# The last four experts write their rows of the output themselves, and the other rows are loaded beside them

## The chip, the cores and the metric

One core of a Trainium2 chip runs the whole program. The metric is the device time of one execution in microseconds. The kernel before takes 1597.99 us (median of 3 runs, 1597.9 to 1598.13).

## The reference

One decoder layer over 2048 tokens of width 1024, in float32: a gated-linear-attention mixer with a residual, then a mixture of experts with a residual, then a final RMSNorm. What matters here is the second half. Each token chooses one of 8 groups and, in it, 2 of 8 experts:

```python
hid = jax.nn.silu(xb @ w1[e]) * (xb @ w3[e])      # xb: the rows of expert e, 1024 -> 256
ys = (hid @ w2[e]) * slot_gate[:, None]           # 256 -> 1024
out = zeros.at[slot_tok].add(ys)                  # two experts a token
x = x + out
return rmsnorm(x, final_norm)                     # each row by its own mean square
```

With 64 experts and 4096 assignments, an expert has 64 rows on average. A row of the result can be normalised once both of its experts have been added.

## The kernel before

The first 930 us are attention and routing; the change does not touch them. They leave four things in DRAM or SBUF: `s["X"]`, the residual stream in DRAM; `s["h"]`, its normalised rows in DRAM; `tok`, a column per expert with the token numbers of its first 96 rows (a number past 2047 where there are fewer); and `s["gate"]`, the factors.

`phase_moe` runs iterations e = 0 to 64, expert by expert, in an order in which neighbours are of different groups (`ORDER`), so that 8 experts in a row share no token. The order of instructions on every engine is the order in which the program writes them. Iteration e scales and scatters the result of expert e-2 (`down` on ACT, `scatter`: an indirect DMA on POOL that adds rows into `s["X"]`), multiplies expert e by its first weights (`up`, twice 12 matmuls), transposes the hidden rows of e-1 (`htrans`), transposes the input rows of e+1 (`xtrans`), gathers the rows of e+4 (`gather`: an indirect DMA on POOL), splits the next weights into two parts (ACT makes the high part on L1157, DVE the low part on L1160), and multiplies expert e-1 by its second weights (`down_mm`, 12 matmuls). Weights come in pieces of 1 MB on SP's queue, up to 11 ahead, into 19 wide slots that `Experts` hands out (`fetch`, `split`, `use`).

An indirect DMA reads its row numbers from SBUF; POOL makes its descriptors, and the DMA engines carry the rows.

After the loop, `phase_more` is a loop over overflow blocks (experts with more than 96 rows); with these inputs it runs no iteration, but entering and leaving it is work for all engines. Then `phase_tail` loads all 16 tiles of `s["X"]` on SP's queue, takes mean squares on ACT (`square`, L1401), the inverse root with one Newton step (`root`, `refine`), multiplies on DVE (`norm`, L1422, with `gf`, the final norm's gain, in SBUF) and stores to `out` on SP's queue (L1423).

Lines that come up below: L67 is the low part of a split whose input is in PSUM, L1222 the product of the two halves of the hidden rows (one input in PSUM), L1004 the scatter of routing entries into a table, L1192 and L1246 the gather and the scatter-add of an expert.

Of the kernel before, what the change touches and what calls it, by code (L numbers as in the profile page):

```python
# [21 lines left out]
S = 2048  # L22
# [35 lines left out]
NTAIL = 29  # L58
# [1112 lines left out]
def phase_moe(tc, c, a, s, ex, plan, rest):  # L1171
    nc = tc.nc
    with ExitStack() as ctx:
# [10 lines left out]
        scat = []  # L1184
# [55 lines left out]

        def down(e):
            Y[e] = ys[e % YS]
            nc.scalar.activation(Y[e][0:CAP, :], PD[e][0:CAP, :], AF.Copy, scale=s["gate"][0:CAP, ORDER[e]:ORDER[e] + 1])  # L1243

        def scatter(e):
            st = nc.gpsimd.indirect_dma_start(  # L1246
                out=s["X"], out_offset=bass.IndirectOffsetOnAxis(ap=tok[:, ORDER[e]:ORDER[e] + 1], axis=0),
                in_=Y[e], in_offset=None, bounds_check=S - 1, oob_is_err=False, compute_op=OP.add)
            for i, o in enumerate(scat):
# [23 lines left out]
        for e in range(E + 1):  # L1273
            live = e < E
            if e > 1:
                down(e - 2)
                scatter(e - 2)
            if live:
                up(e, 0)
# [16 lines left out]
            if e:  # L1296
                down_mm(e - 1)
            if e == 2:
                s["plan"] = plan_more(tc, s, plan)
        down(E - 1)  # L1300
        scatter(E - 1)


def plan_more(tc, s, one):
# [25 lines left out]
    total = one.tile([1, 1], I32, name="total")  # L1330
    nc.vector.tensor_copy(total, end[0:1, E - 1:E])
# [4 lines left out]
def phase_more(tc, c, a, s, slots):  # L1336

    nc = tc.nc
    with ExitStack() as ctx:
        ps = ctx.enter_context(tc.tile_pool(name="o_ps", bufs=1, space=PSUM, reuse_waits="tile"))  # L1340
        ident = c["ident"]
        tl, total, tab = s["plan"]
        w = [slots.tile(F32) for _ in range(6)]
        x, xt, y, small = own = [slots.tile(F32) for _ in range(4)]
        hid, ht = small[:, 0:FF], small[:, FF:2 * FF]
        nc.vector.memset(x, 0.0)
        n = nc.values_load(total[0:1, 0:1], min_val=0, max_val=E)
        with tc.For_i(0, n, 1) as i:
            SP = [mybir.EngineType.SP]
            e = nc.values_load(tl[0:1, bass.ds(i * 2, 1)], engines=SP, min_val=0, max_val=E - 1)  # L1350
            b = nc.values_load(tl[0:1, bass.ds(i * 2 + 1, 1)], engines=SP, min_val=0, max_val=(SLOTS - CAP) // MORE - 1)
            for k in range(6):
                nc.sync.dma_start(w[k], a["w_moe"][bass.ds(e, 1), k // 2, :, k % 2 * D:(k % 2 + 1) * D].rearrange("o p f -> p (o f)"))
            nc.sync.dma_start(tab, s["table"][CAP * E:].rearrange("(b p e) w -> b p e w", p=MORE, e=E)[
                bass.ds(b, 1), :, bass.ds(e, 1), :].rearrange("b p e w -> p (b e w)"))
            nc.gpsimd.indirect_dma_start(
                out=x, out_offset=None, in_=s["h"], in_offset=bass.IndirectOffsetOnAxis(ap=tab[:, 0:1], axis=0),
                bounds_check=S - 1, oob_is_err=False)
            for j in range(2):
                p = ps.tile([128, 512], F32, name="p", bufs=2)  # L1360
                for k in range(4):
                    nc.tensor.transpose(p[:, k * 128:(k + 1) * 128], x[:, (4 * j + k) * 128:(4 * j + k + 1) * 128], ident)
                nc.scalar.activation(xt[:, j * 512:(j + 1) * 512], p, AF.Copy)
            pu = ps.tile([128, 512], F32, name="pu")
            for k in range(NK):
                nc.tensor.matmul(pu, xt[:, k * 128:(k + 1) * 128], w[k // 2][:, k % 2 * 512:(k % 2 + 1) * 512],
                                 start=(k == 0), stop=(k == NK - 1))
            nc.scalar.activation(hid, pu[:, 0:FF], AF.Silu)
            nc.vector.tensor_tensor(hid, hid, pu[:, FF:], op=OP.mult)
            p = ps.tile([128, 256], F32, name="pt")  # L1370
            for k in range(2):
                nc.tensor.transpose(p[:, k * 128:(k + 1) * 128], hid[:, k * 128:(k + 1) * 128], ident)
            nc.scalar.activation(ht, p, AF.Copy)
            for j in range(2):
                p = ps.tile([128, 512], F32, name="p", bufs=2)
                for k in range(2):
                    nc.tensor.matmul(p, ht[:, k * 128:(k + 1) * 128], w[4 + k][:, j * 512:(j + 1) * 512],
                                     start=(k == 0), stop=(k == 1))
                nc.scalar.activation(y[:, j * 512:(j + 1) * 512], p, AF.Copy, scale=tab[:, 1:2].bitcast(F32))
            nc.gpsimd.indirect_dma_start(  # L1380
                out=s["X"], out_offset=bass.IndirectOffsetOnAxis(ap=tab[:, 0:1], axis=0),
                in_=y, in_offset=None, bounds_check=S - 1, oob_is_err=False, compute_op=OP.add)
        slots.free(*w, *own)


def phase_tail(tc, c, a, s, slots, gf):
    nc = tc.nc
    GRP = 4
    with ExitStack() as ctx:
        sm = ctx.enter_context(tc.tile_pool(name="t_sm", bufs=2, side="right", reuse_waits="tile"))  # L1390
        junk = [slots.tile(F32) for _ in range(2)]
        X, SS, R = {}, {}, {}

        def load(t):
            X[t] = slots.tile(F32)
            nc.sync.dma_start(X[t], s["X"][t * 128:(t + 1) * 128, :])

        def square(t):
            if t % GRP == 0:
                SS[t // GRP] = sm.tile([128, GRP], F32, name="ssq")  # L1400
            nc.scalar.activation(junk[t % 2], X[t], AF.Square, accum_out=SS[t // GRP][:, t % GRP:t % GRP + 1])  # L1401

        def root(g):

            v = sm.tile([128, GRP], F32, name="v")
            nc.vector.tensor_scalar(v, SS[g], 1.0 / D, EPS, op0=OP.mult, op1=OP.add)
            y = sm.tile([128, GRP], F32, name="r")
            nc.scalar.activation(y, v, AF.Ln)
            nc.scalar.activation(y, y, AF.Exp, scale=-0.5)
            R[g] = v, y  # L1410

        def refine(g):
            v, y = R[g]
            u = sm.tile([128, GRP], F32, name="u")
            nc.vector.tensor_tensor(u, y, y, op=OP.mult)
            nc.vector.tensor_tensor(u, u, v, op=OP.mult)
            nc.vector.tensor_scalar(u, u, -0.5, 1.5, op0=OP.mult, op1=OP.add)
            nc.vector.tensor_tensor(y, y, u, op=OP.mult)

        def norm(t):  # L1420
            g, i = divmod(t, GRP)
            nc.vector.scalar_tensor_tensor(X[t], X[t], R[g][1][:, i:i + 1], gf, op0=OP.mult, op1=OP.mult)  # L1422
            nc.sync.dma_start(a["out"][t * 128:(t + 1) * 128, :], X[t])  # L1423

        NG = NT // GRP
        for t in range(NT):
            load(t)
        nc.scalar.preload_act_table_set(LN_EXP)
        for t in range(GRP):
            square(t)  # L1430
        root(0)
        refine(0)
        for t in range(GRP, 2 * GRP):
            square(t)
        for g in range(NG):
            if g + 1 < NG:
                root(g + 1)
                for t in range((g + 2) * GRP, min((g + 3) * GRP, NT)):
                    square(t)
            for i in range(GRP):  # L1440
                if i == GRP // 2 and g + 1 < NG:
                    refine(g + 1)
                norm(g * GRP + i)
# [3 lines left out]
def trunk(ctx, tc, a):  # L1447
# [7 lines left out]
        "todo": dram.tile([128, 2], I32, name="s_todo"),  # L1455
        "X": dram.tile([S, D], F32, name="s_X"),
# [22 lines left out]
    with ExitStack() as main:  # L1479
        big = main.enter_context(tc.tile_pool(name="tails", bufs=NTAIL, side="left", reuse_waits="tile"))  # L1480
        slots = Slots()
        slots.add(big, NTAIL)
        gf = slots.tile(F32)
        nc.sync.dma_start(gf, bass.AP(tensor=a["final_norm"].tensor, offset=a["final_norm"].offset, ap=[[0, 128], [1, D]]))
        phase_more(tc, c, a, s, slots)
        phase_tail(tc, c, a, s, slots, gf)
# [41 lines left out]
```

## Time and profile before

| what | value |
|---|---|
| timed runs, median | 1597.99 us |
| profiled execution | 1600.11 us |
| its span, first to last instruction | 1598.3 us |
| PE busy | 1514.1 us (95%) |
| DVE busy | 1096.7 us (69%) |
| ACT busy | 957.0 us (60%) |
| POOL busy | 365.9 us (23%) |
| granted TensorE clock, mean | 0.974 |

The busy shares are means over the whole span. The profile's rows are read by stage: attention and routing to about 930 us, the experts to 1546 us, the tail to the end. A row of an engine's timeline gives the start, the length and the instruction; what stands in brackets is the idle time ahead of it and what ended it. The end of an instruction of POOL that issues a DMA is the end of its descriptors, not the landing of the data.

### The profile page before, as it was taken

The numbers are of one execution on the slowest core, as the hardware profiler recorded it, in microseconds if no ns is written. First come the engines' busy times: TensorE is split into PE (matmuls) and PEld (weight loads), VectorE is DVE, ScalarE is ACT, GpSimd is POOL, SyncE is SP. The second block draws the span as 40 slices with busy tenths as digits, with TensorE's granted clock in tenths as the row PEclk, the third lists the DMA queues.
The fourth block names the chain that finished last, engine by engine and source line by source line (L and its number), as shares of the span: only waits on it lengthen the run. The fifth ranks groups of instructions, "written<-read, shape, count | busy, mean of one in ns | idle before, by whom it ended". The sixth has DMA issues, their size and how long they took to land.

```text
span 1598.3 us, 21450 instructions
## 1 busy us (share of the span) xinstructions
PE 1514.1 (95%) x7619; PEld 1197.2 (75%) x7619; DVE 1096.7 (69%) x2087; ACT 957.0 (60%) x1498; POOL 365.9 (23%) x265
## 2 busy tenths in 40 slices
PE   9999999999999999998999969999999999999960
PEld 7877888888888888877888856777777777777740
DVE  5566665566556655553655558889998998989955
ACT  6666644454445544441222238888888888888854
POOL 3211000000000000130111144535444444454320
PEclk9999999999999999999999979999999999999985
DMA  8645944434333433347488556999999999999969
GB/s 305 227 158 200 341 144 150 145 139 181 120 117 138 174 123 124 132 138 265 174 278 276 212 218 237 386 391 396 390 390 394 394 396 393 386 393 394 392 189 392
DMA packets 113213, 415.24 MB, mean 260 GB/s; under 512 B 23585, under 2 KB 40066, under 8 KB 88530
## 3 DMA queue, kind: packets, MB, share of 16 engines
q1 hardware_dynamic: 90242, 379.72, 61.3%
q0 software_dynamic: 19744, 33.85, 8.4%
q8 instruction: 60, 0.98, 0.2%
q10 hardware_dynamic: 3120, 0.30, 0.2%
q14 instruction: 47, 0.39, 0.1%
HBM read 353.92 MB, written 93.41 MB: 280 GB/s over the span
## 4 chain that ended last, share of the span: by engine, by line
PE 88%; DVE 5%; DMA 3%; ACT 2%; issue 1%; SPq 0%; POOL 0%; DVEq 0%; POOLq 0%; ACTq 0%
PE pm L832 9%; PE pu L77 7%; PE pu L76 7%; PE pu L75 7%; PE pvr L75 7%; PE pvr L76 7%; PE pvr L77 7%; PE pd L76 4%; PE pd L75 4%; PE pd L77 4%; PE ptr L1203 3%; PE pk L75 2%; PE pq L75 2%; PE pq L76 2%; PE pq L77 2%; PE pk L76 2%
## 5 line engine op out<-in xcount | busy, mean ns | idle before, releaser
L1160 DVE TENSOR_TENSOR wide<-wide 128x2048 fp32r<-128x2048 f32 x192 | 435.0, 2286 | 55.4 <-ACT wide L1157 46.8
L1157 ACT ACTIVATE wide<-wide 128x2048 fp32r<-128x2048 f32 x192 | 362.7, 1908 | 6.8 <-PE pd L76 6.4
L1246 POOL DMA_INDIRECT s_X<-y,tok x64 | 187.5, 2929 | 297.8 <-ACT y L1243 283.3
L75 PE MATMUL pu<-wide,xhi 128*96 128x512 f32 x512 | 207.0, 404 | 0.9 <-ACT xhi L66 0.9
L76 PE MATMUL pu<-wide,xhi 128*96 128x512 f32 x512 | 202.5, 396 | 2.2 <-DVE wide L1160 2.2
L77 PE MATMUL pu<-wide,xlo 128*96 128x512 f32 x512 | 203.6, 398 | 0.0
L75 PE MATMUL pvr<-big 128*128 128x512 f32 x504 | 201.2, 399 | 0.0
L76 PE MATMUL pvr<-big 128*128 128x512 f32 x504 | 197.1, 391 | 0.0
L77 PE MATMUL pvr<-big 128*128 128x512 f32 x504 | 196.8, 391 | 0.0
L832 PE MATMUL pm<-big 128*128 128x512 f32 x672 | 163.4, 399 | 5.4 <-DVE big L910 5.4
L67 POOL TENSOR_TENSOR big<-big 128x1024 fp32r<-128x1024 f32 x16 | 39.3, 2468 | 517.6 <-ACT big L66 458.2
L832 PEld LDWEIGHTS pm<-big 128*128 128x128 f32 x672 | 126.0, 191 | 31.4 <-DVE big L910 5.8
L77 PEld LDWEIGHTS pu<-wide,xlo 128*96 128x96 f32 x512 | 83.2, 162 | 36.7 <-DVE xlo L67 0.6
L75 PEld LDWEIGHTS pvr<-big 128*128 128x128 f32 x504 | 94.6, 188 | 20.5
L77 PEld LDWEIGHTS pvr<-big 128*128 128x128 f32 x504 | 94.6, 188 | 20.3
L76 PEld LDWEIGHTS pu<-wide,xhi 128*96 128x96 f32 x512 | 83.7, 164 | 34.5 <-DVE wide L1160 2.9
L66 ACT ACTIVATE sp<-st 128x256 fp32r<-128x256 f32 x64 | 26.7, 417 | 136.5 <-DVE st L455 124.4
L76 PEld LDWEIGHTS pvr<-big 128*128 128x128 f32 x504 | 94.7, 188 | 18.0
L75 PEld LDWEIGHTS pu<-wide,xhi 128*96 128x96 f32 x512 | 83.3, 163 | 32.6 <-ACT xhi L66 1.2
L75 PE MATMUL pd<-wide,ht 128*96 128x512 f32 x256 | 100.8, 394 | 1.3 <-ACT ht L66 1.3
L77 PE MATMUL pd<-wide,ht 128*96 128x512 f32 x256 | 100.7, 393 | 0.0
L76 PE MATMUL pd<-wide,ht 128*96 128x512 f32 x256 | 100.6, 393 | 0.0
(298 smaller groups left out, 2860.6 us busy)
## 6 DMA issues: line engine op xcount, KB each, us to landing
wide<-w_moe SPq DMA_DIRECT2D x192, 1024.0 KB
big<-s_hT SPq DMA_DIRECT2D x96, 512.0 KB
s_hT<-big SPq DMA_DIRECT2D x32, 512.0 KB
s_oT<-big SPq DMA_DIRECT2D x32, 512.0 KB
big<-s_oT SPq DMA_DIRECT2D x32, 512.0 KB
big<-x SPq DMA_DIRECT2D x20, 512.0 KB
big<-w_vr SPq DMA_DIRECT2D x16, 512.0 KB
s_X<-big SPq DMA_DIRECT2D x16, 512.0 KB
```

The lines of the kernel that those rows point to most:

```text
L66: nc.scalar.activation(hi, src, AF.Copy)
L67: eng.tensor_tensor(lo, src, hi.bitcast(F32), op=OP.subtract)
L75: nc.tensor.matmul(out, x[0], w[0], start=start, stop=False)
L76: nc.tensor.matmul(out, x[0], w[1], start=False, stop=False)
L77: nc.tensor.matmul(out, x[1], w[0], start=False, stop=stop)
L832: self.nc.tensor.matmul(pm[i], xo[:, sl], w[:, i * 512:(i + 1) * 512], start=(k == 0 and w is whi and xo is hi), stop=(k == NK - 1 and xo ...
L1157: self.nc.scalar.activation(hi, r, AF.Copy)
L1160: self.nc.vector.tensor_tensor(lo, r, hi.bitcast(F32), op=OP.subtract)
L1203: nc.tensor.transpose(p[:, k, 0:CAP], x[0:CAP, k * 128:(k + 1) * 128], ident[0:CAP, 0:CAP])
L1246: st = nc.gpsimd.indirect_dma_start(out=s["X"], out_offset=bass.IndirectOffsetOnAxis(ap=tok[:, ORDER[e]:ORDER[e] + 1], axis=0), in_=Y[e], ...
```

## The change

The tail and the overflow loop move into `phase_moe`, and the last four experts (60 to 63, one each of four groups) are treated apart.

- `targets` (end of iteration 3) and `targets_in` (end of iteration 6) make `dst`: the row numbers 0 to 2047, with those that any of the last four experts touches replaced by a number past the end. It is stored to DRAM, overwritten there by four indirect DMAs, loaded again as 16 rows of 128, transposed by PE and copied by DVE.
- `xgather` (iterations 60 and 61) gathers from `s["X"]` the rows of experts 60 to 63, and `final` (DVE) adds the gated result to them in SBUF, in place of `down` and `scatter`.
- `load_final` (from iteration 61) loads the tiles of `s["X"]` in pairs into wide slots as these come free.
- Squares begin in iteration 63; after the loop the tiles are normalised, and each is stored by `put_out`, an indirect DMA on POOL with the row numbers `dst`, so that rows of the last four experts are left out. These come from `final_norm`, stored by `put_out` with the expert's own row numbers.
- The overflow loop now stands behind all stores, inside a loop that runs once if there is any overflow; it would redo the tail.

```diff
+        def targets():
+            nc.gpsimd.iota(rows, pattern=[[1, 128]], base=0, channel_multiplier=128, allow_small_or_imprecise_dtypes=True)
+            nc.gpsimd.memset(none, NSENT)
+            nc.gpsimd.dma_start(s["dst"].rearrange("(t p) w -> t (p w)", p=128), rows)
+            for e in range(E - LAST, E):
+                st = nc.gpsimd.indirect_dma_start(
+                    out=s["dst"], out_offset=bass.IndirectOffsetOnAxis(ap=tok[:, ORDER[e]:ORDER[e] + 1], axis=0),
+                    in_=none, in_offset=None, bounds_check=S - 1, oob_is_err=False)
...
+        def targets_in():
+            nc.gpsimd.dma_start(rows, s["dst"].rearrange("(t p) w -> t (p w)", p=128))
+            p = ps.tile([128, 2, 128], F32, name="pht")
+            nc.tensor.transpose(p[:, 0, 0:NT], rows, ident[0:NT, 0:NT])
+            nc.vector.tensor_copy(dst, p[:, 0, 0:NT])
...
+        def final(e):
+            f = fin[e][0:CAP, :]
+            nc.vector.scalar_tensor_tensor(f, PD[e][0:CAP, :], s["gate"][0:CAP, ORDER[e]:ORDER[e] + 1], f, op0=OP.mult, op1=OP.add)
...
+        def load_final():
+            left = len(ex.order) - ex.done
+            while len(XP) < NT // 2 and len(ex.slots) > (left + 1 if left else 0):
...
+                j = len(XP)
+                XP[j] = ex.tile(F32)[0].rearrange("p (i d) -> p i d", i=2)
+                nc.sync.dma_start(XP[j], s["X"][256 * j:256 * (j + 1), :].rearrange("(i p) d -> p i d", p=128))
...
+        def put_out(x, index):
+            st = nc.gpsimd.indirect_dma_start(
+                out=a["out"], out_offset=bass.IndirectOffsetOnAxis(ap=index, axis=0),
+                in_=x, in_offset=None, bounds_check=S - 1, oob_is_err=False)
...
+        def norm(t):
+            g, i = divmod(t, GRP)
+            x = XP[t // 2][:, t % 2, :]
+            nc.vector.scalar_tensor_tensor(x, x, R[g][1][:, i:i + 1], s["gf"], op0=OP.mult, op1=OP.mult)
+            if MASK:
+                put_out(x, dst[:, t:t + 1])
...
-            if e > 1:
+            if 1 < e < E - LAST + 2:
                 down(e - 2)
                 scatter(e - 2)
+            elif e > 1:
+                final(e - 2)
...
             if live:
                 up(e, 1)
                 act(e)
+            if e == E - 1:
+                nc.scalar.preload_act_table_set(LN_EXP)
...
             if e:
                 down_mm(e - 1)
+            if e > E - LAST + 1:
+                final_square(e - 2)
+            if e > E - LAST:
+                load_final()
+            if e == E - 1:
+                square(0)
+                square(1)
             if e == 2:
                 s["plan"] = plan_more(tc, s, plan)
-        down(E - 1)
-        scatter(E - 1)
+            elif e == 3:
+                targets()
+            elif e == 6:
+                targets_in()
+        square(2)
+        square(3)
+        root(0)
+        refine(0)
+        norm(0)
+        final(E - 1)
+        norm(1)
...
+        for g in range(1, NT // GRP):
+            refine(g)
+            for i in range(GRP):
+                t = (g + 1) * GRP + i
+                if t < NT:
+                    square(t)
+                if i == GRP - 1 and g + 1 < NT // GRP:
+                    root(g + 1)
+                norm(g * GRP + i)
+                if len(fs) < LAST and i % 2:
+                    fs.append(final_norm(E - LAST + len(fs)))
```

`MASK` is True. The steps between norm(1) and the loop are the squares of tiles 4 to 7 and of expert 63, the root and refine of the four experts and the root of the second group, interleaved with norms 2 and 3.

## Rows read from the trace of the kernel before

**Rows 1.** Busy time by stretch: us, busy per engine (instructions), PEclk, DMA share, GB/s.

```profile
980.00:1500.00 520.00, 519.71 (x2615) 375.57 (x2614) 470.13 (x354) 453.46 (x398) 242.95 (x116) 1.00 1.01 387
1530.00:1546.30 16.30, 15.01 (x66) 9.96 (x64) 11.18 (x9) 9.02 (x11) 4.82 (x2) 1.00 0.39 70
1569.70:1597.20 27.50, 0.00 (x0) 0.00 (x0) 19.82 (x30) 8.61 (x20) 0.00 (x0) 0.50 0.99 401
```

**Rows 2.** The chain that ended last, from 1538 us: start us, us, what.

```profile
1547.68 5.71 DMA s_X<-y,tok
...
1575.30 7.30 DMA out<-big
```

**Rows 3.** SP's issues at the end: start us, us, instructions merged.

```profile
1554.05 13.39 SPq L1396 DMA_DIRECT2D big<-s_X  x16
1569.77 20.58 SPq L1423 DMA_DIRECT2D out<-big  x16
```

**Rows 4.** POOL's DMAs by line: duration ns least/median/longest, first and last start us.

```profile
L1192 POOL DMA_INDIRECT xb<-s_h,tok x64: 1014/1040/4256, 940.6 to 1502.4; - x64
...
L1246 POOL DMA_INDIRECT s_X<-y,tok x64: 1554/3072/4158, 977.6 to 1547.7; - x64
...
L1004 POOL DMA_INDIRECT s_table<-ent,addr x32: 953/958/1105, 758.0 to 956.2; - x32
...
L219 POOL DMA_DIRECT2D big<-w_a x1: 944/944/944, 5.3 to 5.3; - x1
```

**Rows 5.** POOL's timeline, iterations 3 to 6, and the scatter of expert 59.

```profile
989.61 1.04 POOL L1192 DMA_INDIRECT xb<-s_h,tok  x1 [0.30 <-issue]
995.36 4.16 POOL L1246 DMA_INDIRECT s_X<-y,tok  x1 [4.71 <-ACT y L1243]
...
1018.60 2.57 POOL L1192 DMA_INDIRECT xb<-s_h,tok  x1 [0.30 <-issue]
...
1517.31 3.05 POOL L1246 DMA_INDIRECT s_X<-y,tok  x1 [6.06 <-ACT y L1243]
```

**Rows 6.** DVE's timeline, the same iterations.

```profile
993.58 4.47 DVE L1160 TENSOR_TENSOR wide<-wide 128x2048 fp32r<-128x2048 f32 x2
...
1002.22 4.48 DVE L1160 TENSOR_TENSOR wide<-wide 128x2048 fp32r<-128x2048 f32 x2
...
1020.51 4.48 DVE L1160 TENSOR_TENSOR wide<-wide 128x2048 fp32r<-128x2048 f32 x2
```

**Rows 7.** PE's timeline: two matmuls at the lower clock, the end of iteration 6.

```profile
955.34 0.63 PE L75 MATMUL pu<-wide,xhi 128*96 128x512 f32 x1
955.77 0.63 PE L76 MATMUL pu<-wide,xhi 128*96 128x512 f32 x1
...
1020.43 0.39 PE L77 MATMUL pd<-wide,ht 128*96 128x512 f32 x1
```

**Rows 8.** Busy time by stretch around a PE wait of 4.6 us.

```profile
945.50:950.10 4.60, 0.00 (x0) 0.01 (x1) 3.07 (x2) 0.00 (x0) 4.38 (x3) 0.73 1.00 411
950.10:957.90 7.80, 6.88 (x20) 4.46 (x21) 0.96 (x1) 0.81 (x1) 6.67 (x12) 0.50 0.93 376
```

**Rows 9.** ACT's and DVE's timelines at the end.

```profile
1539.16 1.90 ACT L1157 ACTIVATE wide<-wide 128x2048 fp32r<-128x2048 f32 x1
...
1542.66 0.32 ACT L66 ACTIVATE ht<-pht 128x192 fp32r<-128x192 f32 x1
...
1582.58 7.26 DVE L1422 SCALAR_TENSOR_TENSOR big<-big,r 128x1024 f32<-128x1024 f32 x6
```

**Rows 10.** Groups by line from 1553.5 us: busy us, mean ns.

```profile
L1422 DVE SCALAR_TENSOR_TENSOR big<-big,r 128x1024 f32<-128x1024 f32 x16 | 19.6, 1278 | 0.0
L1401 ACT ACTIVATE big<-big 128x1024 f32<-128x1024 f32 x16 | 16.8, 1048 | 3.5 <-DMA big<-s_X 3.0
L1401 ACT ACTIVATION_READ_ACCUMULATOR big<-big 128x1 f32 x16 | 3.0, 187 | 0.0
L1428 ACT ACT_TABLE_LOAD x1 | 1.3, 1283 | 6.7 <-DMA s_X<-y,tok 6.7
```

More of the change, by code (lines that the diff above doesn't have):

```diff
@@ L1183, in phase_moe @@
         spacer = wk.tile([1, 2], F32, name="spacer2", bufs=1)
-        scat = []
+        scat, outs, xg = [], [], []
+        rows = xp.tile([NT, 128], F32, name="rows")
+        none = xp.tile([128, 1], F32, name="none")
         XT, HID, UP, HT, PD, Y = {}, {}, {}, {}, {}, {}
@@ new lines, in targets_in, with xgather @@
+        def targets_in():
[3 more added lines that the diff above has]
+            nc.vector.tensor_copy(dst, p[:, 0, 0:NT])
+        def xgather(e):
+            st = nc.gpsimd.indirect_dma_start(
+                out=fin[e], out_offset=None, in_=s["X"],
+                in_offset=bass.IndirectOffsetOnAxis(ap=tok[:, ORDER[e]:ORDER[e] + 1], axis=0),
+                bounds_check=S - 1, oob_is_err=False)
+            for i, o in enumerate(scat):
+                if i % GR != e % GR:
+                    tc.declare_no_dep(st.ins, o.ins, reason="experts of different groups share no token")
+            xg.append((e, st))
@@ new lines, in square, with root @@
+        def square(t):
+            g, i = divmod(t, GRP)
+            nc.scalar.activation(junk, XP[t // 2][:, t % 2, :], AF.Square, accum_out=stats[:, g, i:i + 1])
+        def root(g):
+            v = wk.tile([128, GRP], F32, name="v")
+            nc.vector.tensor_scalar(v, stats[:, g, :], 1.0 / D, EPS, op0=OP.mult, op1=OP.add)
+            y = wk.tile([128, GRP], F32, name="r")
+            nc.scalar.activation(y, v, AF.Ln)
+            nc.scalar.activation(y, y, AF.Exp, scale=-0.5)
+            R[g] = v, y
@@ new lines, in refine @@
+        def refine(g):
+            v, y = R[g]
+            u = wk.tile([128, GRP], F32, name="u")
+            nc.vector.tensor_tensor(u, y, y, op=OP.mult)
+            nc.vector.tensor_tensor(u, u, v, op=OP.mult)
+            nc.vector.tensor_scalar(u, u, -0.5, 1.5, op0=OP.mult, op1=OP.add)
+            nc.vector.tensor_tensor(y, y, u, op=OP.mult)
+        def put_out(x, index):
+            st = nc.gpsimd.indirect_dma_start(
+                out=a["out"], out_offset=bass.IndirectOffsetOnAxis(ap=index, axis=0),
+                in_=x, in_offset=None, bounds_check=S - 1, oob_is_err=False)
+            for o in outs:
+                tc.declare_no_dep(st.ins, o.ins, reason="a row of out is written by its last expert or with its tile")
+            outs.append(st)
@@ L1248, in scatter @@
                 in_=Y[e], in_offset=None, bounds_check=S - 1, oob_is_err=False, compute_op=OP.add)
-            for i, o in enumerate(scat):
+            for i, o in list(enumerate(scat)) + xg:
                 if i % GR != e % GR:
@@ new lines, in phase_moe @@
+        root(0)
[3 more added lines that the diff above has]
+        norm(1)
+        square(4)
+        final_square(E - 1)
+        root(4)
+        square(5)
+        refine(4)
+        norm(2)
+        square(6)
+        norm(3)
+        square(7)
+        root(1)
+        fs = []
+        for g in range(1, NT // GRP):
[9 more added lines that the diff above has]
+                    fs.append(final_norm(E - LAST + len(fs)))
@@ new lines, in phase_moe @@
+        if not MASK:
+            for i, f in enumerate(fs):
+                put_out(f, tok[:, ORDER[E - LAST + i]:ORDER[E - LAST + i] + 1])
+        tl, total, tab = s["plan"]
+        ws = [ex.tile(F32)[0] for _ in range(3)]
+        x = ex.tile(F32)[0]
+        x, xt = x[:, 0:D], x[:, D:]
+        y = ex.tile(F32)[0]
+        y, hid, ht = y[:, 0:D], y[:, D:D + FF], y[:, D + FF:D + 2 * FF]
+        some = nc.values_load(total[0:1, 1:2], min_val=0, max_val=1)
+        n = nc.values_load(total[0:1, 0:1], min_val=0, max_val=E)
@@ new lines, in phase_moe @@
+        with tc.For_i(0, some, 1):
+            for e in range(E - LAST, E):
+                nc.gpsimd.indirect_dma_start(
+                    out=s["X"], out_offset=bass.IndirectOffsetOnAxis(ap=tok[:, ORDER[e]:ORDER[e] + 1], axis=0),
+                    in_=fin[e], in_offset=None, bounds_check=S - 1, oob_is_err=False)
+            nc.vector.memset(x, 0.0)
+            with tc.For_i(0, n, 1) as i:
+                block(tc, a, s, i, ps, c["ident"], tl, tab, ws, x, xt, y, hid, ht)
+            for t in range(NT):
+                xs = XP[t // 2][:, t % 2, :]
+                nc.sync.dma_start(xs, s["X"][t * 128:(t + 1) * 128, :])
+                square(t)
+            nc.scalar.preload_act_table_set(LN_EXP)
+            for g in range(NT // GRP):
+                root(g)
+                refine(g)
+                for i in range(GRP):
+                    xs = XP[2 * g + i // 2][:, i % 2, :]
+                    nc.vector.scalar_tensor_tensor(xs, xs, R[g][1][:, i:i + 1], s["gf"], op0=OP.mult, op1=OP.mult)
+                    t = g * GRP + i
+                    nc.sync.dma_start(a["out"][t * 128:(t + 1) * 128, :], xs)
@@ L1338, in phase_more @@
     nc = tc.nc
[L1339 to L1383, printed above, removed]
@@ L1386, in phase_tail @@
[L1386 to L1443, printed above, removed]
@@ new lines, in block @@
+    w = [t[:, k * D:(k + 1) * D] for t in ws for k in range(2)]
+    SP = [mybir.EngineType.SP]
+    e = nc.values_load(tl[0:1, bass.ds(i * 2, 1)], engines=SP, min_val=0, max_val=E - 1)
+    b = nc.values_load(tl[0:1, bass.ds(i * 2 + 1, 1)], engines=SP, min_val=0, max_val=(SLOTS - CAP) // MORE - 1)
+    for k in range(6):
+        nc.sync.dma_start(w[k], a["w_moe"][bass.ds(e, 1), k // 2, :, k % 2 * D:(k % 2 + 1) * D].rearrange("o p f -> p (o f)"))
+    nc.sync.dma_start(tab, s["table"][CAP * E:].rearrange("(b p e) w -> b p e w", p=MORE, e=E)[
+        bass.ds(b, 1), :, bass.ds(e, 1), :].rearrange("b p e w -> p (b e w)"))
@@ new lines, in block @@
+    nc.gpsimd.indirect_dma_start(
+        out=x, out_offset=None, in_=s["h"], in_offset=bass.IndirectOffsetOnAxis(ap=tab[:, 0:1], axis=0),
+        bounds_check=S - 1, oob_is_err=False)
+    p = ps.tile([128, NK, 128], F32, name="ptr")
+    for k in range(NK):
+        nc.tensor.transpose(p[:, k, :], x[:, k * 128:(k + 1) * 128], ident)
+    nc.scalar.activation(xt, p.rearrange("p k i -> p (k i)"), AF.Copy)
+    pu = ps.tile([128, 512], F32, name="pu", bufs=2)
+    for k in range(NK):
+        nc.tensor.matmul(pu, xt[:, k * 128:(k + 1) * 128], w[k // 2][:, k % 2 * 512:(k % 2 + 1) * 512],
+                         start=(k == 0), stop=(k == NK - 1))
@@ new lines, in block @@
+    nc.scalar.activation(hid, pu[:, 0:FF], AF.Silu)
+    nc.vector.tensor_tensor(hid, hid, pu[:, FF:], op=OP.mult)
+    p = ps.tile([128, 2, 128], F32, name="pht")
+    for k in range(2):
+        nc.tensor.transpose(p[:, k, :], hid[:, k * 128:(k + 1) * 128], ident)
+    nc.scalar.activation(ht, p.rearrange("p k i -> p (k i)"), AF.Copy)
+    p = ps.tile([128, D], F32, name="pd")
+    for j in range(2):
+        for k in range(2):
+            nc.tensor.matmul(p[:, j * 512:(j + 1) * 512], ht[:, k * 128:(k + 1) * 128], w[4 + k][:, j * 512:(j + 1) * 512],
+                             start=(k == 0), stop=(k == 1))
@@ L1446, in trunk @@
+    nc.scalar.activation(y, p, AF.Copy, scale=tab[:, 1:2].bitcast(F32))
+    nc.gpsimd.indirect_dma_start(
+        out=s["X"], out_offset=bass.IndirectOffsetOnAxis(ap=tab[:, 0:1], axis=0),
+        in_=y, in_offset=None, bounds_check=S - 1, oob_is_err=False, compute_op=OP.add)
 @with_exitstack
@@ L1455, in trunk @@
         "todo": dram.tile([128, 2], I32, name="s_todo"),
+        "dst": dram.tile([S, 1], F32, name="s_dst"),
         "X": dram.tile([S, D], F32, name="s_X"),
@@ L1478, in trunk @@
     phase_moe(tc, c, a, s, ex, plan, rest)
[L1479 to L1486, printed above, removed]
 def layout(i):
```

45 lines of the change are left out of this document (41 added, 4 removed).

## The prediction

> **What bounds the kernel now.** I read the page's head first (span 1598.3 us), then busy time by stretch, then the chain of waits at the end, then the queues and engines one by one. From 980 to 1500 us, the loop over experts, PE is busy 519.7 of 520 us at the full clock, with the DMA engines full too [rows 1]. PE sets the pace there: time in which PE waits is not given back. From 1530 to 1546 the DMA engines are only 39% busy, since the last weights have landed; PE still works. From 1570 to 1597 the DMA engines are at 0.99 and 401 GB/s and PE does nothing [rows 1]. The chain of waits [rows 2] shows the same end: the last scatter-add of an expert, 5.71 us from POOL's start to landing, and at the end the stores of out. SP issues the 16 loads from 1554.05 and the 16 stores from 1569.77 [rows 3]. So 8.4 MB are read and 8.4 MB written after the last matmul, one after the other at about 400 GB/s: about 42 us. That is what the change goes for.
>
> **What it removes.** The loads move beside the last three experts, where DMA is free. The weights are in soon after 1530 [rows 1]. The loads wait for the scatter of expert 59, whose descriptors end at 1520.4 [rows 5]; with 4.2 to 7 us to land that is about 1527. They need 21 us at 400 GB/s, share the first of it with weights, and are in by about 1553. The four gathers of X take the place of four scatters on POOL, early enough for their users, and cost nothing more. What is left after the matmuls is one write of out. The before frame has its first store at 1569.77.
>
> **What it adds (a): a PE wait in iteration 6.** targets() at the end of iteration 3 puts one plain DMA, a wait for its landing, and four indirect DMAs on POOL, ahead of all later scatters and gathers. targets_in() at the end of iteration 6 issues a load on POOL and then makes PE transpose what it loads. PE takes its instructions in order, so up(7) stands behind this transpose. When does POOL reach the load?
>
> Here I need what an indirect DMA costs on POOL beside DVE. Unhindered it is 1.04 us (gather, the median), 1.55 (scatter-add, the least), 0.96 (scatter into the table) [rows 4]. But the median scatter-add is 3.07 and the longest gather 4.26 [rows 4]. Laying POOL's times over DVE's explains it: a POOL DMA that starts while L1160 runs ends a fixed time after L1160's end, 1.45 us for a scatter-add and 0.91 for a gather. I laid all 128 gathers and scatters of the loop over DVE so: 54 start clear of L1160 and take the least time, one starts with it and does too, the other 73 end by this rule. Two L1160 back to back (993.58, 4.47 us, end 998.05) hold it through both: the scatter-add of 995.36 takes 4.16 and ends at 999.52 [rows 5, 6]. L67 and L1222, which read PSUM, do not hold it.
>
> With that rule, and 0.30 us between POOL instructions [rows 5], from the gather that ends at 990.65: the plain store ends near 992.5 (0.94 for a DMA of that kind [rows 4]) and lands near 995; the four indirect DMAs end at 999.0, 1000.3, 1002.9 and 1007.6 (the first held until 998.05, the last by the pair at 1002.22 [rows 6]). The scatter of expert 2, at 995.36 before, ends at 1009.5; gather 8 at 1012.0, scatter 3 at 1015.1, gather 9 at 1017.8, scatter 4 at 1021.7, and gather 10, held by the pair at 1020.51 [rows 6], at 1025.9 (before it ended at 1021.17 [rows 5]). The load is issued by 1027.1 and lands near 1029.6; for the landing I take 2.5 us, between nothing and the 4.2 that the last scatter-add needs after POOL is done with it (5.71 less 1.55 [rows 2, 4]; a plain store or load may be quicker). PE was ready at 1020.8 [rows 7]. Wait: 8.8 us; 3.5 if POOL had no backlog at all (gather 10 at its old end, +0.3, +0.94, +1.9 to land), 10.5 with the slow landing. Gathers run three experts ahead, and scatters have two more buffers, so the backlog itself stops nobody else.
>
> After a PE wait the granted clock falls. A wait of 4.6 us (945.5 to 950.1) was followed by 7.8 us at the lower level [rows 8], where a matmul takes 0.43 instead of 0.23 us [rows 7]: 15 to 18 matmuls at 0.2 us more, 2.9 to 3.6 us. I take 2.9; the least is 0. Sum of (a): **11.7 us**, bounds 3.5 and 14.
>
> **(b): order on ACT and DVE at the end.** In iteration 63 ACT gets a table load (1.28) ahead of the split at 1539.16, and final_square(61), square(0), square(1) behind it (1.05 each and 0.19 to read the sum) ahead of the copy of htrans(63), which ran at 1542.66 [rows 9, 10]. That copy comes at about 1546.0, and down_mm(63) ends at about 1549.5, not 1546.2: 3.4 us later. It costs little, because normalising tile 0 does not wait for it. final() in place of down() puts 1.3 us more on DVE in iterations 62 and 63; DVE is busy 11.2 of the 16.3 us from 1530 [rows 1], so I take nothing for it (at most 1.3, the whole).
>
> **(c): the tail.** ACT has the squares of tiles 2 and 3 by 1549.5, root and refine take 1.6, the first norm ends at about 1552.3. DVE then has 15 norms and 4 final norms at 1.20 (1.278 long, but six take 7.26 [rows 9, 10]), 22.8 us; final(63) of 1.3; four sets of root and refine of 0.95, and two waits of 0.8 for ACT's logarithm and exponential: 29.5 us, so DVE ends near **1581.8**. ACT, with 1.05 us a square, stays ahead.
>
> The stores no longer go through SP, which issued 16 in 20.6 us beside DVE [rows 3], but are 20 indirect DMAs on POOL. Norms take two inputs from SBUF (X and gf) as L1160 does; no row shows a POOL DMA beside them. Bounds: held by nothing, 1.04 and 0.30 each; or held through every unbroken run of norms. I take the second, the rule of rows 5 and 6. Then POOL gets in only at final(63), at root and at refine: about one store each. By my list it finishes stores 0 to 5, one final, 6 and 7 by 1582.7. Eleven are left, at 1.34 each (1.04 + 0.30): 1597.4; 0.5 MB each in 1.34 us is 390 GB/s, what DMA can carry. Then 4.2 us to land and 0.7 for leaving the loop of the overflow blocks, which now stands behind the stores (the scatter landed at 1553.4, SP's first load left at 1554.05 [rows 2, 3]): end near 1602.3, against 1598.3. Cost of (b) and (c) against the tail of before: **+4.0 us**.
>
> On this the Trainium skill, page "SBUF — State Buffer", section "Who interferes with whom", says two things: that a DVE instruction with two SBUF inputs holds up a GpSimd instruction that reads SBUF, and that tensor_tensor was not seen to stall a GpSimd DMA, because descriptors need only the write side (called inferred there). This case's trace agrees with the first (4.16 us where 1.55 is the least) and not with the second. By the second, the tail would be the free one of rival 2.
>
> **Sum.** 11.7 + 4.0 = 15.7 us, on the span of 1598.3. The profiled execution took 1600.11, the median of the timed runs is 1597.99; the 2 us between them I take as unchanged by the edit. Forecast 1597.99 + 15.7 = 1613.7, **1613 us**.
>
> **Rivals.**
> 1. POOL gets in at each boundary between two norms. For it: norms start 1.20 us apart for 1024 elements, L1160 2.20 for 2048 [rows 6, 9], so a norm leaves more time of its own between two streams. Against: the two pairs in the trace let nothing in. One store then takes two norms, 2.4 us; 12 are out by 1581.8, 8 follow at 1.34: 1592.5 + 4.9 = 1597.4, 0.9 better than before, with (a) 1608.8.
> 2. Norms never hold POOL (or the put-outs start just before each norm). Then the last store follows the last norm: 1581.8 + 1.1 + 4.9 = 1587.8, 10.5 better; with (a) 1599.2, no change that shows.
> 3. The other side: the transpose of iteration 6 finds its rows there, so (a) is nothing to 1, and stores are free as in rival 2: 1588 us. It decides at PE's arrival at 1020.8: the load would have to be issued before about 1018. Against it: gather 10 stands ahead of it on POOL and alone ended at 1021.17 [rows 5]. With only the 3.5 us wait: 1591.
> 4. (a) small (0 to 3.5) and stores held: 1602 to 1606.
>
> **Chances.** Forecast 0.45, rival 1 0.18, rival 2 0.10, rival 3 0.10, rival 4 0.12, something that I do not see 0.05, mostly to the fast side. This kernel's runs agree so closely that 0.2%, 3.2 us, is about the least change that a measurement can tell. Slower by more than that: all of the forecast and rival 1, 0.09 of rival 4, 0.01 of rival 2: 0.73. Within 0.2%: most of rival 2, some of rival 4: 0.11. Faster: 0.16. Range: from rival 3 with a short wait and rival 2 upward, 1594, to the forecast with 14 us in (a) and a slow landing, 1619. The forecast's own range is 1606 to 1618.
>
> **What would show it.** (a) right: in iteration 6 a PE gap of 6 to 10 us that ends with the DMA of the 16-row tile, the lower clock behind it, and the experts after it all later by the same amount; wrong: no gap over 2 us. (b) right: PE's last matmul about 3.4 us after its old place relative to expert 60. (c) right: POOL's stores during the norms 2 to 6 us long and a row of 1.04 us ones after the last norm; wrong: stores that follow each norm within 1.5 us. The loads of X should all have landed before ACT needs them; if the first squares wait for DMA, the gain of the tail shrinks by that wait and the prediction is too low.

## The result and the profile after

The changed kernel takes 1616.68 us (median of 4 runs, 1613.29 to 1618.84), the kernel before 1598.06 beside it: ratio 1.0111, 95% interval 1.0091 to 1.0132, so 18.6 us slower by the medians (17.7 by the ratio). The profiled run took 1615.72 us with a span of 1613.8 [rows 1 to 3 are of a span of 1598.3].

Busy time by stretch, of after (columns as in [rows 1]):

```profile
1016.00:1040.00 24.00, 9.72 (x37) 6.51 (x36) 8.42 (x8) 6.26 (x6) 10.78 (x5) 0.64 0.84 304
1040.00:1510.00 470.00, 470.00 (x2365) 339.50 (x2364) 421.94 (x308) 410.46 (x360) 214.51 (x102) 1.00 1.02 388
1560.00:1570.00 10.00, 5.44 (x12) 3.18 (x12) 6.08 (x10) 7.54 (x17) 0.72 (x1) 0.66 0.79 315
1590.00:1614.00 24.00, 0.00 (x0) 0.00 (x0) 7.96 (x12) 0.41 (x2) 11.33 (x10) 0.50 0.45 177
```

The loop still runs with PE busy throughout, but in one stretch of 24 us PE works for 9.7 us only. SP now issues its loads of X, eight pairs of tiles, beside the last experts:

```profile
1544.74 8.88 SPq L1304 DMA_DIRECT2D wide<-s_X  x8
```

The last 24 us carry 177 GB/s, where [rows 1] had 401. So the reads of X did leave the tail, and PE lost time in the middle.

POOL's timeline in iterations 3 to 6 of after (start us, us; answers to [rows 5]), and PE's at the end of the stop (answers to [rows 7]):

```profile
990.41 0.57 POOL L1257 DMA_DIRECT2D s_dst<-rows  x1 [0.24 <-POOL none L1256]
997.22 1.07 POOL L1260 DMA_INDIRECT s_dst<-none,tok  x1 [6.24 <-DMA s_dst<-rows]
...
1002.35 4.43 POOL L1260 DMA_INDIRECT s_dst<-none,tok  x1 [0.30 <-issue]
...
1021.27 3.90 POOL L1198 DMA_INDIRECT xb<-s_h,tok  x1 [0.30 <-issue]
1025.17 0.58 POOL L1268 DMA_DIRECT2D rows<-s_dst  x1
```

```profile
1034.36 0.25 PE L1270 MATMUL pht<-ident,rows 16*128 16x16 f32 x1 [14.28 <-DMA rows<-s_dst]
...
1035.09 0.63 PE L78 MATMUL pu<-wide,xhi 128*96 128x512 f32 x1
1035.51 0.63 PE L79 MATMUL pu<-wide,xlo 128*96 128x512 f32 x1
```

PE stops for 14.28 us and names the load. POOL had finished issuing it at 1025.75; PE got it 8.6 us later. Behind the stop the matmuls start 0.43 us apart until 1039.2 (the lower level, 1.2 GHz), 4.9 us in all: 11 matmuls at 0.2 us more, about 2.2 us. Over 1020 to 1036 the queues of after carried (packets, MB, share of 16 engines):

```profile
q1 hardware_dynamic: 627, 4.49, 67.5%
q0 software_dynamic: 709, 1.23, 32.4%
```

q0 holds POOL's scatter-adds, its gather and the load; q1 the weights.

The end of after: ACT and DVE around the last matmul (answer to [rows 9]).

```profile
1555.89 1.28 ACT L1411 ACT_TABLE_LOAD   x1
1557.19 1.91 ACT L1159 ACTIVATE wide<-wide 128x2048 fp32r<-128x2048 f32 x1
...
1562.41 0.31 ACT L68 ACTIVATE ht<-pht 128x192 fp32r<-128x192 f32 x1
```

```profile
1559.13 2.29 DVE L1162 TENSOR_TENSOR wide<-wide 128x2048 fp32r<-128x2048 f32 x1 [2.81 <-ACT wide L1159]
1561.34 1.27 DVE L1286 SCALAR_TENSOR_TENSOR y<-pd,gate,y 96x1024 f32<-96x1024 f32 x1
...
1567.72 1.28 DVE L1338 SCALAR_TENSOR_TENSOR wide<-wide,r 128x1024 f32<-128x1024 f32 x1
...
1593.20 4.89 DVE L1338 SCALAR_TENSOR_TENSOR wide<-wide,r 128x1024 f32<-128x1024 f32 x4
```

POOL's stores of out in after (the SP stores of [rows 3] are gone), some of 20:

```profile
1569.28 1.81 POOL L1328 DMA_INDIRECT out<-wide,dst  x1 [23.62 <-DVE wide L1338]
...
1593.76 1.58 POOL L1328 DMA_INDIRECT out<-wide,dst  x1 [0.30 <-issue]
1595.64 0.98 POOL L1328 DMA_INDIRECT out<-wide,dst  x1 [0.30 <-issue]
1596.93 2.02 POOL L1328 DMA_INDIRECT out<-wide,tok  x1 [0.31 <-DVE wide L1338]
...
1603.10 0.98 POOL L1328 DMA_INDIRECT out<-wide,dst  x1 [0.31 <-issue]
```

The last four norms run without a break from 1593.20 to 1598.09, and yet two stores end inside that run. The last store ends 6.0 us behind the last norm. After it come 9.7 us more: 3.6 until POOL's drain at the program's end starts, 5.2 of the drain, and 0.9 behind it. The drain in after and in before (duration ns least/median/longest, first and last start):

```profile
L1641 POOLq DRAIN  x3: 46/105/5220, 1607.7 to 1613.5; - x3
```

```profile
L1524 POOLq DRAIN  x3: 46/105/3219, 1554.2 to 1598.0; - x3
```

In before the long drain (3.22 us) starts at 1554.2, beside the loads of X; in after it is 5.22 us long and starts at 1607.7, when all else is done.

### The profile page after: what moved, and what is told of

The parts are those of the page before. It is cut to its first block, busy times and chain, and to the rows that moved or that the text cites. A ratio compares the mean times of both kernels' runs of the same rounds, so it can differ in the third digit from the quotient of the medians.

```text
span 1613.8 us, 21515 instructions
## 1 busy us (share of the span) xinstructions
PE 1519.5 (94%) x7620; PEld 1199.8 (74%) x7620; DVE 1106.7 (69%) x2102; ACT 958.9 (59%) x1504; POOL 403.2 (25%) x293
## 4 chain that ended last, share of the span: by engine, by line
PE 87%; DVE 6%; DMA 3%; ACT 2%; issue 1%; POOL 0%; DVEq 0%; SPq 0%; POOLq 0%; ACTq 0%
PE pm L834 9%; PE pu L78 7%; PE pu L77 7%; PE pu L79 7%; PE pvr L77 7%; PE pvr L78 7%; PE pvr L79 7%; PE pd L78 4%; PE pd L77 4%; PE pd L79 4%; PE ptr L1209 3%; PE pk L77 2%; PE pq L77 2%; PE pq L78 2%; PE pq L79 2%; PE pk L78 2%
## 5 line engine op out<-in xcount | busy, mean ns | idle before, releaser
L1359 POOL DMA_INDIRECT s_X<-y,tok x60 | 175.3, 2922 | 264.7 <-ACT y L1356 256.2
L77 PE MATMUL pd<-wide,ht 128*96 128x512 f32 x256 | 101.9, 398 | 4.2 <-ACT ht L68 4.2
L1198 POOL DMA_INDIRECT xb<-s_h,tok x64 | 89.3, 1395 | 55.9 <-DVE seen L1000 19.8
L78 PE MATMUL pd<-wide,ht 128*96 128x512 f32 x256 | 101.6, 397 | 0.0
```

The lines of the kernel that those rows point to most:

```text
L77: nc.tensor.matmul(out, x[0], w[0], start=start, stop=False)
L78: nc.tensor.matmul(out, x[0], w[1], start=False, stop=False)
L1198: nc.gpsimd.indirect_dma_start(out=xbs[e % XBS], out_offset=None, in_=s["h"], in_offset=bass.IndirectOffsetOnAxis(ap=tok[:, ORDER[e]:ORDER ...
L1359: st = nc.gpsimd.indirect_dma_start(out=s["X"], out_offset=bass.IndirectOffsetOnAxis(ap=tok[:, ORDER[e]:ORDER[e] + 1], axis=0), in_=Y[e], ...
```

## The experiments

**Iteration 6.** First the row targets alone, in the kernel before, their result unused:

```
+            elif e == 3:
+                targets()
+            elif e == 6:
+                targets_in()
```

> The kernel before with targets() and targets_in() alone, in the same iterations as in the change; the row numbers they make are not used, and the tail is that of before. Theory (the PE wait of iteration 6 is most of the loss): a PE gap of about 14 us that ends with the DMA of the 16-row tile, the lower clock behind it, and a span about 17 us over that of before, near 1615 us. Rival (the loss sits in the tail of the change): a gap, but the span less than 5 us over that of before.

1614.66 us in one run against 1598.0, span 1612.9 against [rows 1]'s run of 1598.3. What PE's stop waited for:

```profile
L1273 POOL DMA_DIRECT2D rows<-s_dst x1: 570/570/570, 1024.2 to 1024.2; - x1
...
  DMA rows<-s_dst: 14.2, 1
```

A helper that touches none of the tail brings nearly the whole loss. Next, the full change with the load left in iteration 6 and only its use moved three experts later:

```
             elif e == 6:
                 targets_in()
+            elif e == 9:
+                targets_turn()        # the transpose and the copy, out of targets_in()
```

> The changed kernel with the load of the row numbers left in iteration 6 and the transpose and copy put three iterations later. Theory: no PE wait over 2 us in iterations 6 or 9 and no fall of the clock, 14.3 + 2.5 us less: span near 1597 us, just under that of before. Rival (POOL's backlog holds the experts elsewhere, so the wait only moves): a gap of several us appears in iteration 7 to 9 and the span stays above 1605 us.

1600.27 us, ratio 1.0012 (1.0003 to 1.0022), span 1598.3. The 14 us wait is gone, and the span is 1.3 us above the 1597 expected. The transpose now waits for PE's own work only:

```profile
L1268 POOL DMA_DIRECT2D rows<-s_dst x1: 570/570/570, 1024.8 to 1024.8; - x1
...
  PE pd L78: 0.4, 1
```

POOL's backlog is unchanged (the load at 1024.8, at 1025.2 before the move), and no wait of PE hangs on it. One wait is left, 1.14 us: `htrans` needs the one `pht` tile, out of which DVE copies `dst` only after other work.

```profile
1051.42 0.38 PE L1233 MATMUL pht<-ident,hid 96*128 96x96 f32 x2 [1.14 <-DVE dst L1273]
```

So the stop of PE is 16.4 us of the 18.6 (1616.68 less 1600.27). Everything else in the change, this 1.14 us with it, is +2.3 us by the medians, +1.9 by the ratio (+0.5 to +3.5 by its interval). Then the whole of targets_in() in iteration 20, where POOL has no backlog:

```
-            elif e == 6:
+            elif e == 20:
                 targets_in()
```

> The changed kernel with load, transpose and copy together in iteration 20, when POOL has no backlog left. Theory (half of the wait was backlog, half the slow landing behind the scatter and the gather that stand ahead on POOL's DMA queue): POOL issues the load about 1 us before PE is there and it takes 8 to 9 us to land, so PE waits 7 to 8 us instead of 14.3; span near 1605 us. Rival (the landing takes 2.5 us as I predicted, and the backlog was the rest): PE waits under 2.5 us, span near 1599 us.

1608.5 us in one run. The tile of rows, by line, and PE's wait:

```profile
L1268 POOL DMA_DIRECT2D rows<-s_dst x1: 577/577/577, 1145.0 to 1145.0; - x1
...
L1270 PE MATMUL pht<-ident,rows x1: 256/256/256, 1155.8 to 1155.8; 16*128 16x16 f32 x1
...
  DMA rows<-s_dst: 8.8, 1
```

PE waits 8.8 us, above the 7 to 8 expected. It is 10.2 us from the end of the issue to the transpose, right behind a gather issued at 1143.97. The slow landing is not the backlog's. Is it POOL's queue or the busy DMA engines? The same, issued by ACT:

```
-            nc.gpsimd.dma_start(rows, s["dst"]...)
+            nc.scalar.dma_start(rows, s["dst"]...)
```

> The rows' load, transposes and copy together in iteration 20, as in the run where POOL issued the load right behind a gather and the transposes waited 8.8 us (issue ended 1145.60, transpose 1155.8: 10.2 us); here the same load is issued by ACT, on a queue that nothing else uses. Theory (the load's packets stand behind those of POOL's gather and scatter in POOL's queue): from ACT's issue to the transpose takes 2 to 4 us. Rival (the weight stream on the shared DMA engines holds any small load): again 8 to 10 us. Either way PE waits for it if ACT reaches the issue late, so the issue's end to the transposes is what tells, not the span.

```profile
L1268 ACTq DMA_DIRECT2D rows<-s_dst x1: 345/345/345, 1144.7 to 1144.7; - x1
...
L1270 PE MATMUL pht<-ident,rows x1: 202/202/202, 1150.0 to 1150.0; 16*128 16x16 f32 x1
...
  DMA rows<-s_dst: 2.8, 1
```

1602.5 us in one run. The issue ends at 1145.1, the transpose comes 4.9 us later: half of 10.2, and above the 2 to 4 expected. So about half of the long landing goes with POOL's queue. The record of DMA packets shows where the time goes, since only the load's 16 rows are packets of 512 B (counted under 2 KB but not under 512 B). The run with POOL's load, from 1145.6 to 1153.5 and on to 1155; then the run with ACT's, from 1148.1 to 1149:

```profile
DMA packets 626, 3.02 MB, mean 383 GB/s; under 512 B 199, under 2 KB 199, under 8 KB 315
DMA packets 133, 0.66 MB, mean 442 GB/s; under 512 B 37, under 2 KB 53, under 8 KB 53
```

```profile
DMA packets 68, 0.28 MB, mean 310 GB/s; under 512 B 8, under 2 KB 24, under 8 KB 46
```

On POOL's queue none of the 16 moves for 7.9 us after the issue. In that time 116 packets of 4 KB (315 less 199) go by, rows of the scatter-add and the gather that POOL had issued before. On ACT's queue all 16 start between 1148.1 and 1149, 3.1 us and more after the issue, while POOL's rows are still moving. This fits the order within POOL's queue. Why the first packet takes 3.1 us even on a queue of its own, these runs do not tell.

**The tail.** gf copied to a PSUM tile, so that a norm reads one input from SBUF and one from PSUM (on top of the moved transpose, as are the runs that follow):

```
+        gp = ps.tile([128, D], F32, name="ptr")
+        nc.vector.tensor_copy(gp, s["gf"])
-  scalar_tensor_tensor(x, x, R[g][1][:, i:i + 1], s["gf"], ...)
+  scalar_tensor_tensor(x, x, R[g][1][:, i:i + 1], gp, ...)
```

> As the version with the later transpose, and the norm's gain copied into PSUM before the tail, so that the norms and final norms read one input from SBUF and one from PSUM. Theory (a DVE instruction with two inputs from SBUF holds an indirect DMA on POOL until its end): all 20 stores take about 1 us each, none 1.6 to 2.0, and POOL ends about 1.5 us after the last norm instead of 6.0; span 4 to 5 us under the version with the gain in SBUF, near 1592 us. Rival (any DVE work holds POOL, or POOL is slow by itself): stores of 1.6 to 2.0 us remain and the span is the same within 1 us.

1596.21 us, ratio 0.9988 (0.9978 to 0.9998), span 1594.1. The stores by form, with the last norms (four from 1577.10, 4.86 us, end 1581.96), and the drain:

```profile
L1330 POOL DMA_INDIRECT out<-wide,dst x16: 975/977/1014, 1553.3 to 1582.5; - x16
L1330 POOL DMA_INDIRECT out<-wide,tok x4: 975/975/977, 1565.2 to 1577.0; - x4
...
L1648 POOLq DRAIN  x3: 46/105/5220, 1588.1 to 1593.9; - x3
```

No store is longer than 1.01 us (up to 2.02 before the edit), and the last ends 1.5 us behind the last norm, not 6. The span fell by 4.2 us, as expected, though to 1594.1 and not 1592. So norms do hold POOL's stores, by their second SBUF input. On this the Trainium skill, page "SBUF — State Buffer", section "Who interferes with whom", says that a DVE instruction with two SBUF inputs holds up a GpSimd instruction that reads SBUF; the run agrees (2.02 us with two, 1.01 with one). This version is faster than both kernels, than the one before only by 0.1%. Then, with gf in SBUF again, the 16 stores on SP with row numbers left out, so that rows of the last four experts are written twice, and the four expert stores on POOL behind them:

```
-MASK = True
+MASK = False
```

> The version with the later transpose, with MASK False: the 16 tiles are stored whole by SP, and the four experts' rows are stored over them by POOL afterwards. Theory: the tiles' stores follow the norms and nothing holds them, but the four last stores wait for the landing of the 16 (about 1586 us), then 4 x 1.3 us, 2 us to land, and the exit of the loop and POOL's drain of 5.2 us as before: span near 1600 us, 0 to 3 us over the version with the later transpose alone. Rival (POOL's drain lasts in proportion to the indirect DMAs ahead of it): drain under 2 us, span near 1596 us.

1601.85 us, ratio 1.0024 (1.0015 to 1.0034): no better than POOL's stores. POOL's four stores came last (1590.15 to 1595.04), then a drain of 3.9 us, neither the 5.2 of the theory nor the rival's under 2:

```profile
L1645 POOLq DRAIN  x3: 46/105/3913, 1597.8 to 1602.3; - x3
```

Next, the overflow loop left out, on top of gf in PSUM; with these inputs it runs no iteration, but a program for any inputs needs it:

```
-        with tc.For_i(0, some, 1):
...
```

> The version with the gain in PSUM, without the overflow loop at the end (it would handle experts with more than 96 rows; with these inputs it runs no iteration). Theory (the loop makes all engines wait for every landing and only then lets POOL drain): POOL drains beside the last landings, 4 us less, span near 1590 us. Rival (the drain begins only when POOL's DMAs have landed, loop or not): only the 1.0 us of semaphore waits goes, span near 1593 us.

1591.56 us, ratio 0.995 (0.9933 to 0.9966), span 1590.8. POOL's last store and the drain:

```profile
1582.66 0.98 POOL L1330 DMA_INDIRECT out<-wide,dst  x1 [0.31 <-issue]
```

```profile
L1617 POOLq DRAIN  x3: 46/98/7841, 1582.2 to 1590.5; - x3
```

From the last store's end to the end of the span are now 7.2 us where there were 10.6. The drain starts at 1582.2, even ahead of the last store, and ends at 1590.0; with the loop it had started at 1588.1, behind the landing. It still ends 3.3 us after SP's own drain starts (1586.7), which I take for the last landing that SP saw. The span lost 3.3 us, nearer the theory's 4 than the rival's 1.

**The order on ACT and DVE.** ACT's copy of htrans(63) ahead of the squares:

```
+            if e == E:                 # behind the copy of htrans(63)
+                final_square(e - 3); square(0); square(1)
```

> The version with the gain in PSUM, with final_square(61), square(0) and square(1) put behind ACT's copy of the transposed hidden rows of expert 63. Theory: the last matmul ends 3.5 to 5 us sooner (the PE gap ahead of it goes from 4.2 us to about 1 us, and the clock does not fall in it), but the first norm waits for the same squares on ACT, so the span is the same within 1 us (1594). Rival (the last matmul is on the path): span 3 to 4 us less, near 1590.5 us.

1595.87 us, ratio 0.9983 (0.9973 to 0.9992), no change that can be told from the 0.9988. ACT's, DVE's and PE's timelines:

```profile
1544.32 0.31 ACT L68 ACTIVATE ht<-pht 128x192 fp32r<-128x192 f32 x1
```

```profile
1544.44 2.29 DVE L1162 TENSOR_TENSOR wide<-wide 128x2048 fp32r<-128x2048 f32 x1 [2.81 <-ACT wide L1159]
1546.65 1.27 DVE L1288 SCALAR_TENSOR_TENSOR y<-pd,gate,y 96x1024 f32<-96x1024 f32 x1
```

```profile
1548.07 0.71 PE L77 MATMUL pd<-wide,ht 128*96 128x512 f32 x1 [4.22 <-ACT xb L1310]
```

The last matmul came no sooner, so the theory fell, and the rival was not tested. The copy is done 3.4 us before the matmul, and the wait is the 4.2 us that it was: down_mm(63) needs the one pd buffer, which final(62) frees at 1547.92, behind the low part that DVE could not start until ACT's high part behind the table load. The releaser that the row names, an ACT square, neither reads nor writes pd. Two tries to start the norms earlier, the first with squares 0 and 1 in ACT's hole ahead of up(63, 1):

```
+            if e == E - 1:
+                square(0); square(1)
             if live:
                 up(e, 1)
```

> The version with gf in PSUM, with square(0) and square(1) put ahead of up(63, 1), where ACT sits idle for 2.43 us (1537.12 to 1539.55) instead of behind the table load and the high part. In the version without this edit ACT works without a break from 1539.55 to 1550.08, and root, refine and the first norm (1551.78) hang on its fourth square. Theory (the tail's start hangs on that row of ACT, not on PE's last matmul): the fourth square ends 2 x 1.2 = 2.4 us earlier, the first norm starts about 1549.4, final(63) may then wait up to 0.7 us for the last matmul (about 1551.1); the span falls by 1.7 to 2.4 us, to 1591.7 to 1592.4 from 1594.1, and the time to about 1594. Rival (the tail hangs on PE's last matmul or on the loads of X): the first norm and the span move by less than 0.7 us.

1596.61 us, ratio 0.9984 (0.9975 to 0.9994): the theory fell. ACT's timeline:

```profile
1539.16 1.06 ACT L1310 ACTIVATE xb<-wide 128x1024 f32<-128x1024 f32 x1 [0.74 <-DMA wide<-s_X]
...
1548.59 1.06 ACT L1292 ACTIVATE xb<-y 96x1024 f32<-96x1024 f32 x1 [2.35 <-issue]
```

square(0) waits for X, and ACT then stands for 2.35 us until final(62) lets final_square(62) go, with squares 2 and 3 queued behind. The hole only moved. So final_square(62) behind them:

```
         square(2)
         square(3)
+        final_square(E - 2)            # was ahead of them
```

> As the version with square(0) and square(1) in ACT's hole ahead of up(63, 1), but with final_square(62) moved behind square(2) and square(3). In that version ACT stood still for 2.35 us (1546.23 to 1548.59) for final(62), with square(2) queued behind it, and the first norm came at 1553.61, no earlier than without the edit. Theory (squares 2 and 3 were held in ACT's queue behind an operation that waits for DVE): they end by about 1548.7 on that run's clock, the root follows, and the first norm starts about 1551.4, 2.2 us earlier; the span falls by 1.5 to 2.2 us against the version with gf in PSUM (1594.1), to 1592 to 1592.6, and the time's ratio to before goes from 0.9988 to about 0.9975. Rival (the end of the tail hangs on the number of norms behind the last matmul, not on the first one's start, since final(63) must wait for the last matmul and the later squares then wait for DVE): the first norm starts earlier, but the last store ends within 0.7 us of where it did.

1596.87 us, ratio 0.9993 (0.9984 to 1.0002). DVE's timeline:

```profile
1550.80 1.28 DVE L1340 SCALAR_TENSOR_TENSOR wide<-wide,r,ptr 128x1024 f32<-128x1024 f32 x1
1553.45 1.28 DVE L1288 SCALAR_TENSOR_TENSOR xb<-pd,gate,xb 96x1024 f32<-96x1024 f32 x1 [1.38 <-PE pd L79]
```

The first norm does start 1.0 us earlier than with gf in PSUM alone (1551.78), but final(63), next on DVE, waits 1.38 us for PE's last matmul (1553.4, where it had been 1551.1), and the last store ends at 1584.0 instead of 1583.5: the rival. The squares, final(62) and the last matmul come within 2 us of each other; moving one hands the start to the next.

## Why the prediction was right, and where its terms were off

The forecast, 1613, was 3.7 us under the time. Its sign and its larger cause hold. The sum 11.7 + 4.0 = 15.7 was 16.4 + 2.3 = 18.7 by the medians (18.6 measured in one piece): one term 4.7 too small, above its own upper bound of 14, the other 1.7 too large.

**(a), the wait in iteration 6.** The order of POOL's work came out as worked: the four indirect DMAs were to end at 999.0, 1000.3, 1002.9 and 1007.6, and the last ended at 1006.78; the load was to be issued by 1027.1 and was by 1025.75. The rule of [rows 5, 6] stands for these, with luck in the first: it was to be held by DVE until 998.05, but took 1.07 us unheld at 997.22, because the store of the row numbers kept POOL waiting 6.2 us and not 2.5. The step that failed is "for the landing I take 2.5 us, between nothing and the 4.2": it took 8.6, and 10.2 in the run without a backlog. The upper bound was the landing of a scatter-add when POOL's queue and the weights had run dry [rows 2]; this load stood behind a scatter-add and a gather, under the weight stream, and that is no such row. The trace of before had one: the wait of [rows 8] is for a gather in the weight stream, whose descriptors were done 1.06 us after its start, so that 8.3 us are its landing.

```profile
940.60 9.38 DMA xb<-s_h,tok
```

PE's gap of 14.28 us lay outside the 6 to 10 named as the sign. The clock's term, 2.9 from [rows 8], was about 2.2. With the landing right the term would have been 14.9 + 2.2.

**(b), the last matmul.** Taken as 3.4 us later and off the path. It ended 5.5 us later (1551.7 with the transpose moved, 1546.2 before): PE was 1.1 us late from iteration 9, the wait was 4.2 us where 1.25 had stood, and the first matmuls behind it ran at the lower level (in after the clock of the stretch from 1560 is 0.66). The cause named, ACT's copy, was one of two that ended together; the other, final(62) on DVE, I had taken as nothing. Off the path is right, but narrowly: in after the last matmul ends at 1568.2, and final(63), which needs it, starts behind the first norm at 1568.92. Where the first norm came sooner, the last matmul held final(63) up by 1.38 us.

**(c), the tail.** DVE's stretch was right: 30.4 us from the first norm to the last, worked out as about 30.7. Two steps failed against each other, and that (c) came near is luck. "I take the second" (held through every unbroken run of norms): the run of four norms above lets a store in at each boundary. A store that starts within 0.05 us of a norm's start takes 0.98; one that starts later ends about 0.85 us after that norm (the first store, beside final(63), fits neither). Rival 1 had the boundaries, but 8 stores left at DVE's end, where 5 were and the forecast had 11. The stores of 0.98 to 2.02 us are neither the 2 to 6 us named as the sign nor free. The last store ended at 1588.6 (transpose moved) where 1597.4 stood: 8.8 us better. That the norms hold nothing at all (rival 2) is wrong too, by 4.2 us of the span (1598.3 against 1594.1 with gf in PSUM). The other step is "4.2 us to land and 0.7 for leaving the loop": it was 9.7, since POOL's drain, left out of the sum, came behind both (3.6 to its start, then 6.1). In before it was hidden, so no chain of waits showed it. Minus 8.8 and plus 4.8 leave 0.0 on the span, where +4.0 stood; by the medians +2.3.

The loads of X were in time for the squares of after, as forecast; only when these were moved ahead did one wait (0.74 and 1.59 us).

So the expected gain, some 21 us of reads out of the tail, went elsewhere. The first norm in before, and with the transpose moved:

```profile
1568.46 2.48 DVE L1422 SCALAR_TENSOR_TENSOR big<-big,r 128x1024 f32<-128x1024 f32 x2
```

```profile
1552.22 1.28 DVE L1340 SCALAR_TENSOR_TENSOR wide<-wide,r 128x1024 f32<-128x1024 f32 x1
```

It starts 16.2 us sooner. From it to the end of the last norm DVE takes 30.4 us where it took 21.4 (1589.84 in before), with four final norms, final(63) and waits for ACT in between. From there to the end of the span are 15.7 us where there were 8.5: stores held behind norms, the loop and the drain. 16.2 less 9.0 less 7.2 is nothing, and PE's stop took 16.4 us on top.

## What to carry to other kernels

Where a small load feeds an instruction on the engine that sets the pace, ask first how far ahead it is issued: three experts' distance saved 16.4 us, with the same instructions. For its landing, take a row from a queue as loaded as the one it will use, and count what stands ahead of it there. When the last work moves to another engine or queue, read that engine's closing instructions in the trace before too: what is hidden there may come last afterwards.

## What was not expected of the hardware

- A load of 8 KB on POOL's queue landed 8.6 and 10.2 us after its issue in the middle of the weight stream; the same load issued by ACT landed within 4.9. The moving itself took about 1 us each time.
- The drain that POOL runs at the program's end takes 3.2 to 7.8 us in these traces. Behind the loop it took 5.2 us after 20 indirect stores and 3.9 after four; what sets its length is not shown.
- One operand moved from SBUF to PSUM, at the same 1.20 us between norms, freed 20 POOL stores: 2.02 us at most became 1.01.
